# Retention scores of two heads as one 256-column product in high and low halves, with one transpose for both heads' keys

## The chip, the cores and the metric

The kernel runs on one core of a Trainium2 chip. A core has a matrix engine (TensorE, PE in the profile), a vector engine (VectorE, DVE), a scalar engine (ScalarE, ACT), GpSimd (POOL) and SyncE (SP), which here only issues DMAs. Each engine works through its own list in order and waits on semaphores. The metric is device microseconds of one execution; the median of three runs is compared.

## The reference

One encoder layer with 1,024 positions of width 1,024. After a modulated RMS norm one input projection feeds two groups of heads: eight retention heads and eight heads of latent attention. Both outputs go through one output projection and a gated residual. The change is in the retention. Its reference, cut to what matters:

```python
# q, k: (B,H,S,64) after rotary embedding, v: (B,H,S,128); chunks of 128 positions
scores = jnp.einsum('bhnik,bhnjk->bhnij', qc, kc) * decay_intra[None, :, None]
intra = jnp.einsum('bhnij,bhnjv->bhniv', scores, vc)
k_decay = jnp.exp(log_gamma[:, None] * (CHUNK - 1 - idx)[None])
kv_chunk = jnp.einsum('bhnjk,bhnjv->bhnkv', kc * k_decay[None, :, None, :, None], vc)
# states: scan over chunks; q_decay likewise
cross = jnp.einsum('bhnik,bhnkv->bhniv', qc * q_decay[None, :, None, :, None], states)
return (intra + cross).reshape(B, H, S, dv)
# run once forward (with the diagonal) and once on flipped sequences (without it), and added
```

## The kernel before

Data stay in fp32. Most products use a split: an operand is written as a high half (rounded to the matmul type fp32r) and a low half (the rest), and `mm3` (lines 64 to 67) adds three products, high by high, high by low and low by high. The small products of the retention were left as plain fp32 products, without a split.

The retention loop (lines 330 to 446) takes a pair of heads per pass `g`, four passes. A pass first makes eight tiles `t` of 128 positions. The projection of a tile is 24 products of 512 columns into a PSUM bank `acc` (line 343), giving q and k of both heads (4 x 64 columns) and v. VectorE and GpSimd apply the rotary embedding (lines 354 to 361) and write four blocks of 64 columns into every other row of `r_`, one of two buffers `rbuf` of eight rows: q of the two heads in rows 0 and 2, k in rows 4 and 6. The copy of line 362 doubles the q rows into rows 1 and 3; rows 5 and 7 stay zero.

Then per tile: `kd`, the keys scaled by the forward and the backward decay, in four instructions (line 366); four transposes of two rows each into one PSUM tile `tp` (line 370), giving q of each head twice on the 128 partitions, and k of each head over 64 zeros; a copy of all of it, `qkT` (line 372); `qdT`, q scaled by both decays (line 374); one plain fp32 score product per head (line 378), whose upper 64 partitions meet zeros of k; `sT`, scores times the mask (line 380); the state products of `kd` with v (line 385), added into the running states `ST` (lines 392 and 396). The PSUM tiles `tp`, `scp` and `kv` rotate over four banks (`sm`).

After the eight tiles the gate of the pair is projected (lines 404 to 414), and for each half of the sequence the outputs are made from `sT`, `qdT`, `ST` and v (lines 424 and 425), normalised (lines 430 to 438), transposed (line 442) and multiplied by the gate into `ro` (line 444), which SyncE stores.

`mla_gate` (lines 449 to 461) projects gates of the attention heads; its first two calls use the buffers of `qkT` for their results. The two calls follow the loop in the program, but are run beside its last pass.

The program order is not the order on the chip: when the program is built, a planner (`schedule_with_timeline_sim=True`) plays it through with its own estimate of each instruction's time and fixes every engine's list. So large products of the next tile or pair are listed between a tile's transposes and its scores. The order of the lists is fixed from then on, and an instruction at the head of a list that waits holds all behind it.

Of the kernel before, what the change touches and what calls it, by code (L numbers as in the profile page):

```python
# [18 lines left out]
P = 128  # L19
# [11 lines left out]
def body(tc, I, O):  # L31
# [291 lines left out]
    retD = dram.tile([H, P, S], F32, name="retD")  # L323
    mgD = dram.tile([H, P, S], F32, name="mgD")

    rbuf = [p_ret.tile([P, 8, 64], F32, name=f"rb{i}", tag=f"rb{i}") for i in range(2)]
    for b_ in rbuf:
        G.memset(b_, 0.0)

    for g in range(4):  # L330
        w = w0 if g == 0 else [wpage(I["w_ret"][g][j], 1024, 2) for j in range(4)]
        vv = []
        ST = p_ret.tile([P, NT, 2, P], F32, name="ST", tag="ST")
        sT = [None] * NT
        qdT = [None] * NT
        for t in range(NT):
            if g == 0 and t < NB0:
                ps = acc0[t]
            else:
                ps = acc()  # L340
                for k in range(KT):
                    wh, wl = w[k // 2]
                    mm3(ps, hh[k][:, ts_(t)], hl[k][:, ts_(t)], wh[:, k % 2], wl[:, k % 2], k == 0, k == KT - 1)
            v_ = p_ret.tile([P, 2, P], F32, name="v", tag="v", bufs=9)
            A.copy(out=v_.rearrange("p h d -> p (h d)"), in_=ps[:, 256:512])  # L345
            vv.append(v_)
            xq = ps[:, 0:256]
            if g == 0 and NACC <= t < NB0:
                xq = p_ret.tile([P, 256], F32, name="xq", tag="o", bufs=5)
                A.copy(out=xq, in_=ps[:, 0:256])  # L350
            xq = xq.rearrange("p (a d) -> p a d", d=32)
            t1 = p_ret.tile([P, 4, 2, 32], F32, name="t1", tag="t1", bufs=2)
            t2 = p_ret.tile([P, 4, 2, 32], F32, name="t2", tag="t2", bufs=2)
            V.tensor_tensor(out=t1.rearrange("p a b d -> p (a b) d"), in0=xq,
                            in1=Cr[:, t:t + 1].broadcast_to([P, 8, 32]), op=ALU.mult)
            V.tensor_tensor(out=t2.rearrange("p a b d -> p (a b) d"), in0=xq,
                            in1=Sr[:, t:t + 1].broadcast_to([P, 8, 32]), op=ALU.mult)
            r_ = rbuf[t % 2]
            rv = r_.rearrange("p (a z) d -> p a z d", z=2)[:, :, 0].rearrange("p a (b d) -> p a b d", b=2)
            G.tensor_tensor(out=rv[:, :, 0], in0=t1[:, :, 0], in1=t2[:, :, 1], op=ALU.subtract)  # L360
            G.tensor_tensor(out=rv[:, :, 1], in0=t1[:, :, 1], in1=t2[:, :, 0], op=ALU.add)
            V.tensor_copy(out=r_[:, 1:4:2], in_=r_[:, 0:4:2])
            kd = p_ret.tile([P, 2, 2, 64], F32, name="kd", tag="kd", bufs=2)
            for h in range(2):
                for d in range(2):
                    V.tensor_scalar(out=kd[:, h, d], in0=r_[:, 4 + 2 * h],
                                    scalar1=kfac[:, 2 * g + h, d:d + 1], scalar2=None, op0=ALU.mult)
            tp = sm(512)
            for a in range(4):
                T.transpose(tp[:, ts_(a)], r_[:, 2 * a:2 * a + 2].rearrange("p a b -> p (a b)"), ident)  # L370
            qkT_ = p_ret.tile([P, 4, P], F32, name="qkT", tag="qkT", bufs=2)
            A.copy(out=qkT_.rearrange("p a b -> p (a b)"), in_=tp)
            qdT_ = p_ret.tile([P, 2, P], F32, name="qdT", tag="qdT", bufs=8)
            V.tensor_tensor(out=qdT_, in0=tp[:, 0:256].rearrange("p (a b) -> p a b", a=2),
                            in1=qfac[:, 2 * g:2 * g + 2], op=ALU.mult)
            scp = sm(256)
            for h in range(2):
                T.matmul(scp[:, ts_(h)], qkT_[:, 2 + h], qkT_[:, h], start=True, stop=True)
            sT_ = p_ret.tile([P, 2, P], F32, name="sT", tag="sT", bufs=8)
            V.tensor_tensor(out=sT_, in0=scp.rearrange("p (h d) -> p h d", h=2), in1=mask[:, 2 * g:2 * g + 2],  # L380
                            op=ALU.mult)
            sT[t], qdT[t] = sT_, qdT_
            kv = sm(256)
            for h in range(2):
                T.matmul(kv[:, ts_(h)], kd[:, h].rearrange("p a b -> p (a b)"), v_[:, h], start=True, stop=True)
            kvv = kv.rearrange("p (h d) -> p h d", h=2)
            if t < NT - 1:
                if t == 0:
                    V.tensor_copy(out=ST[0:64, 1], in_=kvv[0:64])
                else:  # L390
                    for h in range(2):
                        V.scalar_tensor_tensor(out=ST[0:64, t + 1, h], in0=ST[0:64, t, h],
                                               scalar=gch[0:64, 2 * g + h:2 * g + h + 1], in1=kvv[0:64, h],
                                               op0=ALU.mult, op1=ALU.add)
            if t > 0:
                A.copy(out=ST[64:128, t - 1], in_=kvv[64:128])
        for t in range(NT - 2, 0, -1):
            for h in range(2):
                V.scalar_tensor_tensor(out=ST[64:128, t - 1, h], in0=ST[64:128, t, h],
                                       scalar=gch[64:128, 2 * g + h:2 * g + h + 1], in1=ST[64:128, t - 1, h],  # L400
                                       op0=ALU.mult, op1=ALU.add)


        wg = [wpage(I["w_rg"][g][j], 1024, 4) for j in range(2)]
        sg = p_ret.tile([P, 2, S], F32, name="sg", tag="sg")
        for h in range(2):
            for half in range(2):
                ps = acc()
                for k in range(KT):
                    wh, wl = wg[k // 4]  # L410
                    rh = hh[k][:, half * 512:half * 512 + 512]
                    rl = hl[k][:, half * 512:half * 512 + 512]
                    mm3(ps, wh[:, k % 4, ts_(h)], wl[:, k % 4, ts_(h)], rh, rl, k == 0, k == KT - 1)
                A.activation(sg[:, h, half * 512:half * 512 + 512], ps, AF.Silu)

        for half in range(2):
            mv = p_ret.tile([P, 4, 2, 2], F32, name="mv", tag="mv", bufs=2)
            ob = []
            for q in range(4):
                t = half * 4 + q  # L420
                op = sm(256)
                lo, hi = (64, 128) if t == 0 else (0, 64) if t == NT - 1 else (0, 128)
                for h in range(2):
                    T.matmul(op[:, ts_(h)], sT[t][:, h], vv[t][:, h], start=True, stop=False)  # L424
                    T.matmul(op[:, ts_(h)], qdT[t][lo:hi, h], ST[lo:hi, t, h], start=False, stop=True)  # L425
                o_ = p_ret.tile([P, 2, P], F32, name="o", tag="o", bufs=5)
                A.copy(out=o_.rearrange("p h d -> p (h d)"), in_=op)
                for h in range(2):
                    bs = p_ret.tile([P, 6], F32, name="bs", tag="bs", bufs=4)
                    V.bn_stats(out=bs, in_=o_[:, h])  # L430
                    V.bn_aggr(out=mv[:, q, h], in_=bs)
                ob.append(o_)
            rst = p_ret.tile([P, 4, 2], F32, name="rst", tag="rst", bufs=2)
            rstd(rst.rearrange("p a b -> p (a b)"), mv[:, :, :, 1].rearrange("p a b -> p (a b)"), 8)
            for q in range(4):
                for h in range(2):
                    V.tensor_scalar(out=ob[q][:, h], in0=ob[q][:, h], scalar1=mv[:, q, h, 0:1],
                                    scalar2=rst[:, q, h:h + 1], op0=ALU.subtract, op1=ALU.mult)
            for h in range(2):
                tp = sm()  # L440
                for q in range(4):
                    T.transpose(tp[:, ts_(q)], ob[q][:, h], ident)
                ro = p_ret.tile([P, 512], F32, name="ro", tag="ro", bufs=2)
                V.scalar_tensor_tensor(out=ro, in0=tp, scalar=gnw[:, 2 * g + h:2 * g + h + 1],
                                       in1=sg[:, h, half * 512:half * 512 + 512], op0=ALU.mult, op1=ALU.mult)
                SY.dma_start(out=retD[2 * g + h, :, half * 512:half * 512 + 512], in_=ro)
# [14 lines left out]
                A.dma_start(out=mgD[2 * n + h, :, sl], in_=mo)  # L461

    for n in range(MG0):
        mla_gate(n, p_ret, "qkT")
    rts.close()


# [498 lines left out]
```

## Time and profile before

| | |
|---|---|
| median of three runs | 1058.83 us (1058.5 to 1059.71) |
| the profiled execution | 1057.49 us, of which its span is 1055.3 us |
| mean granted TensorE clock | 0.988 of full speed |
| instructions | 15,223 |
| TensorE's busy time | 1018.1 us |
| retention loop | about 80 to 436 us of the span |

The span runs from the first to the last instruction that the profile shows. Times in rows are microseconds from the span's start. `PE` rows are matmuls, `PEld` rows their weight loads. A matmul's duration reaches into the next one's, so distances between starts tell what it holds the array for. A plain fp32 product is shown as two matmul instructions, a transpose and an fp32r product as one. In a group of instructions "x4" is their count, and in square brackets stands the idle time of the engine ahead of it and what ended it.

### The profile page before, as it was taken

The numbers are of one execution on the slowest core, as the hardware profiler recorded it, in microseconds if no ns is written. First come the engines' busy times: TensorE is split into PE (matmuls) and PEld (weight loads), VectorE is DVE, ScalarE is ACT, GpSimd is POOL, SyncE is SP. The second block draws the span as 40 slices with busy tenths as digits, with TensorE's granted clock in tenths as the row PEclk, the third lists the DMA queues.
The fourth block names the chain that finished last, engine by engine and source line by source line (L and its number), as shares of the span: only waits on it lengthen the run. The fifth ranks groups of instructions, "written<-read, shape, count | busy, mean of one in ns | idle before, by whom it ended". The sixth has DMA issues, their size and how long they took to land.

```text
span 1055.3 us, 15223 instructions
## 1 busy us (share of the span) xinstructions
PE 1018.1 (96%) x5736; PEld 888.3 (84%) x5736; DVE 581.4 (55%) x1390; ACT 426.0 (40%) x800; POOL 404.1 (38%) x311
## 2 busy tenths in 40 slices
PE   5899999999999999999999999989999999989998
PEld 4687887888888888998888889879889999878887
DVE  7996546444643534336302116777877777883342
ACT  6654213312321322124322006577767776772100
POOL 2233315213411411224633217943466555873210
PEclk8899999999999999999999999999999999998999
DMA  9721103101110212224654520100000000003522
GB/s 365 264 64 57 41 1 120 41 2 62 63 36 20 85 47 73 102 84 136 201 171 153 183 85 11 41 1 2 20 21 21 2 20 22 21 20 120 169 101 70
DMA packets 30744, 82.27 MB, mean 78 GB/s; under 512 B 3536, under 2 KB 4560, under 8 KB 30672
## 3 DMA queue, kind: packets, MB, share of 16 engines
q1 hardware_dynamic: 25920, 72.92, 20.4%
q10 hardware_dynamic: 4752, 8.39, 2.2%
q8 instruction: 45, 0.74, 0.3%
q14 instruction: 27, 0.22, 0.1%
HBM read 64.52 MB, written 16.78 MB: 77 GB/s over the span
## 4 chain that ended last, share of the span: by engine, by line
PE 82%; DVE 11%; DMA 2%; ACT 2%; issue 2%; POOL 2%; ACTq 0%; DVEq 0%; POOLq 0%
PE acc L65 13%; PE acc L66 13%; PE acc L67 13%; PE pt L739 4%; PE sp L65 4%; PE sp L66 4%; PE sp L67 4%; PE po L66 3%; PE po L67 3%; PE po L65 3%; DVE x L178 2%; DMA wa<-w_ada 2%; PE sm L425 2%; PE sm L424 1%; PE sm L65 1%
## 5 line engine op out<-in xcount | busy, mean ns | idle before, releaser
L81 POOL TENSOR_TENSOR wl<-wr,wh 128x1024 fp32r<-128x1024 f32 (+2 forms) x51 | 115.2, 2268 | 173.2 <-ACT wh L80 148.9
L65 PE MATMUL acc<-wh,hh 128*128 128x512 f32 (+2 forms) x352 | 130.8, 372 | 1.7 <-ACT hh L189 1.7
L66 PE MATMUL acc<-wl,hh 128*128 128x512 f32 (+2 forms) x352 | 130.3, 370 | 0.0
L67 PE MATMUL acc<-wh,hl 128*128 128x512 f32 (+2 forms) x352 | 126.4, 368 | 2.1 <-DVE hl L190 2.1
L725 POOL TENSOR_SCALAR pr<-pr,st 128x1024 f32<-128x1024 f32 x62 | 72.0, 1165 | 101.1 <-DVE st L724 75.5
L65 PE MATMUL acc<-hh,wh 128*128 128x512 f32 x256 | 101.0, 395 | 1.7 <-ACT v L345 1.7
L742 DVE TENSOR_TENSOR pl<-pt,ph 128x512 fp32r<-128x512 f32 x128 | 85.3, 683 | 31.2 <-ACT ph L741 31.1
L66 PE MATMUL acc<-hl,wh 128*128 128x512 f32 x256 | 100.9, 394 | 0.0
L67 PE MATMUL acc<-hh,wl 128*128 128x512 f32 x256 | 100.6, 393 | 0.0
L80 ACT CAST wh<-wr 128x1024 fp32r<-128x1024 f32 (+2 forms) x55 | 53.8, 982 | 104.1 <-PE sm L66 45.1
L741 ACT CAST ph<-pt 128x512 fp32r<-128x512 f32 x128 | 73.1, 591 | 26.6 <-PE pt L739 24.6
L720 DVE TENSOR_REDUCE st<-sp 128x1 f32<-128x1024 f32 x62 | 75.4, 1216 | 6.5 <-PE sp L67 6.4
L66 PE MATMUL po<-pl,vh 128*128 128x256 f32 x256 | 76.5, 299 | 2.1 <-DVE pl L742 2.0
L723 ACT ACTIVATE pr<-sp,st 128x1024 f32<-128x1024 f32 x62 | 69.5, 1121 | 20.8 <-DVE st L721 20.5
L65 PEld LDWEIGHTS acc<-wh,hh 128*128 128x128 f32 x352 | 67.2, 191 | 10.9 <-ACT hh L189 2.1
L67 PEld LDWEIGHTS acc<-wh,hl 128*128 128x128 f32 x352 | 66.0, 188 | 11.1 <-DVE hl L190 3.0
L66 PEld LDWEIGHTS acc<-wl,hh 128*128 128x128 f32 x352 | 67.3, 191 | 8.7
L739 PE MATMUL pt<-ident,pr 128*128 128x128 f32 x496 | 70.2, 274 | 4.0 <-DVE st L724 2.7
L65 PE MATMUL po<-ph,vh 128*128 128x256 f32 x256 | 73.3, 286 | 0.0
L67 PE MATMUL po<-ph,vl 128*128 128x256 f32 x256 | 72.8, 284 | 0.0
L360 POOL TENSOR_TENSOR rb<-t,t 128x128 f32<-128x128 f32 x32 | 14.8, 464 | 135.0 <-PE sm L370 73.4
L739 PEld LDWEIGHTS pt<-ident,pr 128*128 128x128 f32 x496 | 57.9, 141 | 8.5 <-issue 2.9
(353 smaller groups left out, 2474.2 us busy)
## 6 DMA issues: line engine op xcount, KB each, us to landing
x<-w_ada SPq DMA_DIRECT2D x16, 512.0 KB, 7.1
wr<-w_ret SPq DMA_DIRECT2D x16, 512.0 KB, 3.5
wr<-w_rg SPq DMA_DIRECT2D x8, 512.0 KB, 3.5
retD<-ro SPq DMA_DIRECT2D x16, 256.0 KB, 2.1
wr<-w_mg SPq DMA_DIRECT2D x8, 512.0 KB, 3.5
wa<-w_ada SPq DMA_DIRECT2D x8, 512.0 KB, 3.5
wr<-w_out SPq DMA_DIRECT2D x8, 512.0 KB, 4.5
wro<-retD SPq DMA_DIRECT2D x8, 512.0 KB, 3.9
```

Of the source, the lines that this page charges most:

```text
L65: T.matmul(out, lh, rh, start=first, stop=False, **kw)
L66: T.matmul(out, lh, rl, start=False, stop=False, **kw)
L67: T.matmul(out, ll, rh, start=False, stop=last, **kw)
L80: A.copy(out=hi, in_=raw)
L81: eng.tensor_tensor(out=lo, in0=raw, in1=hi, op=ALU.subtract)
L178: V.scalar_tensor_tensor(out=wa, in0=wa, scalar=1.0, in1=sc, op0=ALU.mult, op1=ALU.mult, accum_out=mp[:, i:i + 1])
L720: V.tensor_reduce(out=st_[:, 0:1], in_=sp, op=ALU.max, axis=AX.X)
L723: A.activation(pr, sp, AF.Exp, bias=st_[:, 1:2], scale=sc_, accum_out=st_[:, 2:3])
L725: G.tensor_scalar(out=pr, in0=pr, scalar1=st_[:, 3:4], scalar2=0.0, op0=ALU.mult, op1=ALU.add)
L739: T.transpose(tp[:, ts_(q)], pr[:, ts_(half * 4 + q)], ident)
L741: A.copy(out=ph[half][:, :, c_], in_=tv)
L742: V.tensor_tensor(out=pl[half][:, :, c_], in0=tv, in1=ph[half][:, :, c_], op=ALU.subtract)
```

## The change

Row 5 of `r_` now also gets a copy (of row 4, the first head's k; the copy of line 362 covers three rows), and the third transpose takes rows 5 and 6, so that both heads' k lie on one set of 128 partitions, the first head on the lower 64 and the second on the upper 64. The fourth transpose is gone. k is split into `kTh` and `kTl`. q is split per head into tiles of 256 columns, `qh_` and `ql_`, kept zero outside two blocks: the first head's q on the lower 64 partitions of the first 128 columns, the second head's on the upper 64 of the last 128. One `mm3` of 256 columns then gives both heads' scores. The keys' decays are applied in one instruction with broadcast operands. `qkT` is gone, the cleared buffers are the q tiles instead of `rbuf`, and the two early calls of `mla_gate` use the buffers of `ro`.

```diff
     rbuf = [p_ret.tile([P, 8, 64], F32, name=f"rb{i}", tag=f"rb{i}") for i in range(2)]
-    for b_ in rbuf:
-        G.memset(b_, 0.0)
+    qz = [[p_ret.tile([P, 2, P], F32R, name=f"qz{n}{i}", tag=f"qz{n}{i}") for n in "hl"] for i in range(2)]
+    for z_ in qz:
+        for b_ in z_:
+            G.memset(b_.bitcast(F32), 0.0)
...
-            V.tensor_copy(out=r_[:, 1:4:2], in_=r_[:, 0:4:2])
+            V.tensor_copy(out=r_[:, 1:6:2], in_=r_[:, 0:5:2])
             kd = p_ret.tile([P, 2, 2, 64], F32, name="kd", tag="kd", bufs=2)
+            V.tensor_tensor(out=kd, in0=r_[:, 4:7:2].unsqueeze(2).broadcast_to([P, 2, 2, 64]),
+                            in1=kfac[:, 2 * g:2 * g + 2].unsqueeze(3).broadcast_to([P, 2, 2, 64]), op=ALU.mult)
+
+            tp = sm(384)
             for h in range(2):
-                for d in range(2):
-                    V.tensor_scalar(out=kd[:, h, d], in0=r_[:, 4 + 2 * h],
-                                    scalar1=kfac[:, 2 * g + h, d:d + 1], scalar2=None, op0=ALU.mult)
-            tp = sm(512)
-            for a in range(4):
-                T.transpose(tp[:, ts_(a)], r_[:, 2 * a:2 * a + 2].rearrange("p a b -> p (a b)"), ident)
-            qkT_ = p_ret.tile([P, 4, P], F32, name="qkT", tag="qkT", bufs=2)
-            A.copy(out=qkT_.rearrange("p a b -> p (a b)"), in_=tp)
+                T.transpose(tp[:, ts_(h)], r_[:, 2 * h:2 * h + 2].rearrange("p a b -> p (a b)"), ident)
+            T.transpose(tp[:, ts_(2)], r_[:, 5:7].rearrange("p a b -> p (a b)"), ident)
             qdT_ = p_ret.tile([P, 2, P], F32, name="qdT", tag="qdT", bufs=8)
             V.tensor_tensor(out=qdT_, in0=tp[:, 0:256].rearrange("p (a b) -> p a b", a=2),
                             in1=qfac[:, 2 * g:2 * g + 2], op=ALU.mult)
+
+            kTh, kTl = (p_ret.tile([P, P], F32R, name=f"kT{n}", tag=f"kT{n}", bufs=1) for n in "hl")
+            A.copy(out=kTh, in_=tp[:, 256:384])
+            V.tensor_tensor(out=kTl, in0=tp[:, 256:384], in1=kTh, op=ALU.subtract)
+            qh_, ql_ = qz[t % 2]
+            for h in range(2):
+                hs = slice(64 * h, 64 * h + 64)
+                A.copy(out=qh_[hs, h], in_=tp[hs, ts_(h)])
+                V.tensor_tensor(out=ql_[hs, h], in0=tp[hs, ts_(h)], in1=qh_[hs, h], op=ALU.subtract)
             scp = sm(256)
-            for h in range(2):
-                T.matmul(scp[:, ts_(h)], qkT_[:, 2 + h], qkT_[:, h], start=True, stop=True)
+            mm3(scp, kTh, kTl, qh_.rearrange("p a b -> p (a b)"), ql_.rearrange("p a b -> p (a b)"), True, True)
...
     for n in range(MG0):
-        mla_gate(n, p_ret, "qkT")
+        mla_gate(n, p_ret, "ro")
```

## Rows read from the trace of the kernel before

**Rows 1.** The page's engine table: busy us (share of the span) and instructions.

```profile
PE 1018.1 (96%) x5736; PEld 888.3 (84%) x5736; DVE 581.4 (55%) x1390; ACT 426.0 (40%) x800; POOL 404.1 (38%) x311
```

**Rows 2.** Windows, one a pass: length, busy PE, PEld, DVE, ACT, POOL; clock; DMA.

```profile
80.00:172.00 92.00, 88.63 (x471) 74.68 (x469) 49.11 (x165) 27.78 (x57) 27.68 (x32) 1.00 0.13 39
...
260.00:347.00 87.00, 87.00 (x466) 74.17 (x465) 44.72 (x149) 21.86 (x41) 25.14 (x27) 1.00 0.15 49
```

**Rows 3.** All of TensorE's waits, 75 to 400 us: total, times, longest.

```profile
PE acc L65 <- ACT v L345: 1.7, 1, 1.7
PE sm L442 <- DVE o L437: 1.7, 2, 1.4
PE sm L378 <- ACT qkT L372: 0.7, 1, 0.7
```

**Rows 4.** Timeline of TensorE, two regular tiles: start, duration, instruction.

```profile
123.71 0.60 PE L370 MATMUL sm<-ident,rb 128*128 128x128 f32 x4
...
129.18 0.60 PE L378 MATMUL sm<-qkT 128*128 128x128 f32 x4
...
130.07 0.60 PE L370 MATMUL sm<-ident,rb 128*128 128x128 f32 x4
130.42 0.48 PE L67 MATMUL acc<-wh,hl 128*128 128x512 f32 x1
130.74 0.40 PE L65 MATMUL acc<-wh,hh 128*128 128x512 f32 x1
130.97 0.40 PE L66 MATMUL acc<-wl,hh 128*128 128x512 f32 x1
```

**Rows 5.** Timeline of TensorE, attention stage, fp32r products of 256 columns.

```profile
831.03 0.28 PE L65 MATMUL po<-ph,vh 128*128 128x256 f32 x1
...
831.74 0.28 PE L65 MATMUL po<-ph,vh 128*128 128x256 f32 x1
831.86 0.60 PE L739 MATMUL pt<-ident,pr 128*128 128x128 f32 x4
832.22 0.37 PE L66 MATMUL po<-pl,vh 128*128 128x256 f32 x1
832.42 0.29 PE L67 MATMUL po<-ph,vl 128*128 128x256 f32 x1
```

**Rows 6.** Timeline of TensorE, first two tiles of the second pair.

```profile
170.57 0.62 PE L370 MATMUL sm<-ident,rb 128*128 128x128 f32 x4
...
172.53 0.61 PE L378 MATMUL sm<-qkT 128*128 128x128 f32 x4
...
173.69 0.60 PE L370 MATMUL sm<-ident,rb 128*128 128x128 f32 x4
174.96 0.71 PE L378 MATMUL sm<-qkT 128*128 128x128 f32 x4 [0.68 <-ACT qkT L372]
```

**Rows 7.** Groups by line and shape, ScalarE and VectorE: busy us, mean ns.

```profile
L742 DVE TENSOR_TENSOR pl<-pt,ph 128x512 fp32r<-128x512 f32 x128 | 85.3, 683 | 31.2 <-ACT ph L741 31.1
...
L366 DVE TENSOR_SCALAR kd<-rb,kfac 128x64 f32<-128x64 f32 x128 | 45.1, 406 | 0.0
...
L372 ACT COPY qkT<-sm 128x512 f32<-128x512 f32 x32 | 18.8, 587 | 87.3 <-PE sm L370 87.3
...
L374 DVE TENSOR_TENSOR qdT<-sm,qfac 128x256 f32<-128x256 f32 x32 | 13.1, 408 | 0.5 <-ACT qkT L372 0.5
...
L427 ACT COPY o<-sm 128x256 f32<-128x256 f32 x32 | 11.5, 374 | 31.7 <-PE sm L425 28.8 <-DVE bs L430 1.1 <-issue 1.0
```

**Rows 8.** Timeline of VectorE: four slow scalings and what follows them.

```profile
267.64 3.22 DVE L366 TENSOR_SCALAR kd<-rb,kfac 128x64 f32<-128x64 f32 x4
270.79 0.41 DVE L374 TENSOR_TENSOR qdT<-sm,qfac 128x256 f32<-128x256 f32 x1
```

**Rows 9.** Timeline of TensorE in the same tile as those scalings.

```profile
266.92 0.60 PE L370 MATMUL sm<-ident,rb 128*128 128x128 f32 x4
...
272.39 0.60 PE L378 MATMUL sm<-qkT 128*128 128x128 f32 x4
```

## The prediction, made before any run of the changed kernel

> **What bounds the kernel now.** The first view to read is the engine table: TensorE is busy for 96% of the span, the next engine, VectorE, for 55% [rows 1]. An average can hide a stage with another limit, so the second view is the windows over the four passes of the retention loop, one pass a pair of heads. From the second pair on TensorE has no idle time at all, VectorE stands at about half and ScalarE at a quarter; the first window, 92.00 us with 88.63 busy, has some [rows 2]. The third view, who TensorE waited for between 75 and 400 us, says how much: 1.7, 1.7 and 0.7 us, 4.1 in all, and each of these waits lies at the start of the loop or at the change from the first pair to the second [rows 3]. So in this stage an instruction taken from TensorE's list shortens the kernel by the time it held the array, and an instruction on another engine costs nothing as long as its result is there before TensorE's list reaches the reader. Both halves of that sentence have to be priced.
>
> **The array time of the removed and added products.** A busy time can't be used here: matmuls overlap, and the durations of 0.60 for four are longer than their spacing. What counts is the distance between starts. In a regular tile the group scores, state products, transposes starts at 129.18 and the large products go on at 130.42, the second of them 0.32 us later instead of the usual 0.23 [rows 4]. From 129.18 to 130.74, less one large product (0.23), is 1.33 us for 12 instructions, 0.111 each; the starts inside the group say the same (129.18 and 130.07: 0.89 for eight). A plain fp32 score product stands as two instructions in the trace, so the two score products are four, 0.445 us, and one transpose is 0.111.
>
> The new score product is three fp32r products of 256 columns. The kernel has such ones in the attention stage: from 831.03 to 831.74 there are six steps, 0.118 each [rows 5]; three are 0.355 us. Mixing the two kinds has no price of its own beyond the late second start counted above: four transposes between 256-column products take from 831.86 to 832.42 less one step of 0.118, 0.44 us, again 0.111 each [rows 5]. A lower bound for a step is half of a 512-column step, 0.113, so 0.340 for three; an upper one is the single step of 0.20 behind transposes [rows 5], which would make 0.355 + 0.08. I take 0.355, the steady row with the same tile shape.
>
> So per tile the scores give 0.445 - 0.355 = 0.09 and the missing transpose 0.11, together 0.20 us. There are 4 x 8 = 32 tiles: **6.4 us** off TensorE's list, with 3.8 (the dear step) and 6.9 (the cheap step) as bounds.
>
> **The other engines' work.** ScalarE's one copy of 128x512 was 0.587 us; a copy of 128x256 is 0.374 [rows 7]. The difference, 0.213 per 256 columns, puts one of 128 columns at 0.267; three of them are 0.80 of busy time, +0.2 us a tile. On VectorE the same step from 0.408 (256 columns out of PSUM) to 0.683 (512) gives 0.27 for a 128-column subtraction; three are 0.81. The four scalings of the decayed keys cost 4 x 0.406 = 1.62 us a tile [rows 7]; the one broadcast product of 256 columns should be near the 0.408 row. The copy that doubles rows has 192 columns instead of 128, under 0.1 more. VectorE so changes by 0.41 + 0.81 + 0.1 - 1.62, about -0.3 us a tile. Neither engine comes near TensorE's 96%, so all this is costed at nothing in itself; TensorE's own products cover it, and without that cover it would be the chain below that counts. Four cleared tiles of 256 columns instead of two of 512 are the same number of columns on GpSimd, which is busy for 38% [rows 1]: nothing. The gate tiles that now share the buffers of the normalised outputs could make ScalarE wait for an output DMA, 2 to 3 us once; four accumulator banks cover that: nothing.
>
> **The added wait, and who stands behind it.** Before, the scores waited for one ScalarE copy. Now the first of the three products waits for both heads' high half, the second for the last subtraction, and the third for the low half of k. On VectorE these stand behind the decayed-query product: 0.41 + 3 x 0.27 = 1.22 us if nothing overlaps, against 0.59 for the copy: the chain from transposes to scores grows by **0.64 us**, and by nothing if the starts overlap well enough. Behind the waiting score product in TensorE's list stand the state products, the next tile's transposes (whose PSUM buffers follow), and then all large products.
>
> Is there room? In 30 of the 32 tiles the scores start 5.47 us after their transposes (123.71 and 129.18 in [rows 4]), the transposes take 0.45, so 5.0 us are left for a chain of about 1.3. The worst case seen is a tile in which the four scalings stood in front on VectorE and took 3.22 us, twice their mean of 1.62: the transposes start at 266.92, the decayed-query product at 270.79, and the scores at 272.39 [rows 8, 9]. With three subtractions, 0.81, behind 271.2, the new chain ends at 272.0, 0.4 us before it is needed. So in the regular pattern the wait stays hidden, though in such tiles only just.
>
> At the start of the second pair the room is gone. The scores follow 1.96 us behind the transposes in the first tile and 1.27 in the second, and there TensorE already waits 0.68 us for the copy [rows 6]. These two tiles I charge with the longer chain: 2 x 0.64 = **1.3 us** lost (bounds: nothing, and 2 x 1.3 if the scaling stands in front too).
>
> A rule bears on the hope that VectorE also gets rid of its slow tiles. Scalings of one size and form have a mean of 0.406 us, but took 3.22 for four in the tile above [rows 7, 8], so part of that time is a wait inside the instruction. The Trainium skill (GPSIMD Engine Reference, Key points) says that GpSimd shares its SBUF interfaces with VectorE and that instructions in a two-port mode, or with two SBUF inputs, contend. By that rule the new scaling, which reads keys and factors both from SBUF, can still be held once a tile, and the 4.1 us of waits would not go away; without it one might count them as an extra gain. I count none of them in the sum.
>
> **Sum.** -6.4 + 1.3 = -5.1 us. The profiled execution took 1057.49 us, 2.2 of them outside its span of 1055.3, and becomes 1052.4. The median of the three runs is 1058.83, 1.34 above that execution, and so the forecast for the median is **1053.7 us**, 0.5% faster. What a measurement here can tell from no change is about 0.2%, 2.1 us.
>
> **The rivals.**
>
> *Everything is got and the old waits go too.* Fewer VectorE instructions at the start of the second pair would remove the waits of 1.7 and 0.7 us for normalised outputs and the copy: -6.4 - 2.4 = -8.8, 1050.0 us. For it speaks the lighter VectorE, against it the rule above and the longer chain at just that place. Chance 0.13.
>
> *No change.* The order of each engine's list is made anew by the planner from its own idea of the times, and the chain from transposes to scores sets how soon the next tile's transposes can be listed. If it lets the scores follow their transposes as closely as in the second pair's first tiles in some ten tiles, ten times 0.64 gives back the 6.4 us; the same happens if the freed array time turns into waits for weights at the pair changes. Time 1056.7 to 1060.9. For it: TensorE did run dry at one pair change, and a loop whose tiles come later leaves less other work beside the outputs. Against it: at the other two pair changes no wait at all is seen [rows 3]. Chance 0.17.
>
> *Slower.* The same mechanism in every tile: scores right behind the transposes in all 32, each waiting 0.64 us longer: 20.5 - 6.4 = +14.1, 1072.9 us. It decides from 13 exposed tiles on (13 x 0.64 = 8.3, less 6.4, is +2). For it: small instructions on two engines that hand over to each other five times, where one copy stood. Against it: the distance of 5.47 us, the same in 30 tiles, leaves 3.7 to spare. Chance 0.10.
>
> *The change doesn't shorten the list*, because a step of 256 columns is dearer between plain fp32 products: the bound of 3.8 us, less 1.3, 1056.3. This lies at the edge of the forecast's own range and is counted in it.
>
> **How the numbers follow.** The forecast has 0.60; its own range is 1051 to 1056.5, from the bounds of the array time (3.8 to 6.9) and of the exposed tiles (0 to 2.6). With the first rival faster has 0.73, the same 0.17, slower 0.10. To leave out no more than 2 in 10 the range goes from 1050.2, where most of the first rival is outside, to 1058.9, past half of the no-change case.
>
> **What would show it.** In the changed kernel's profile: three transposes a tile (96 in all) and 96 score products of 256 columns, with 0.118 us between starts, the whole small group of a tile about 1.13 us instead of 1.33. The distance from transposes to scores should stay above 5 us in most tiles, and TensorE's waits for a subtraction or a small copy should sum to under 3 us. The windows of the later pairs should show TensorE as busy as before and be about 1.6 us shorter each. VectorE's busy time should fall by about 10 us, and ScalarE's rise by about 7. The prediction is wrong if score products show waits in many tiles, if the step is near 0.2, or if new idle time appears at the changes of pairs or in the latent projections after the loop.

## The result, and the profile after

The changed kernel took **1119.99 us** (median of 4 runs, 1119.24 to 1122.44) against 1059.27 for the kernel before on the same chip: a ratio of 1.0575 [1.0553, 1.0596], 5.8% slower where 0.5% faster was forecast. Its profiled execution spans 1120.5 us, 65.2 more than before.

The page's engine table of the changed kernel, to be held against [rows 1]:

```profile
PE 1037.8 (93%) x5672; PEld 899.8 (80%) x5672; DVE 586.6 (52%) x1390; ACT 430.2 (38%) x864; POOL 408.5 (36%) x313
```

TensorE has 64 instructions fewer and yet is busy 19.7 us longer, and its idle time, span less busy, rose from 37.2 to 82.7 us. The two together, 45.5 + 19.7, are the 65.2 us. Where they lie is in the windows over the retention stage of the changed kernel, cut as [rows 2]:

```profile
80.00:172.00 92.00, 85.70 (x424) 72.20 (x423) 43.96 (x143) 25.89 (x68) 22.20 (x27) 0.94 0.09 32
172.00:260.00 88.00, 79.38 (x378) 65.43 (x378) 39.71 (x117) 19.44 (x51) 23.21 (x24) 0.92 0.13 43
260.00:347.00 87.00, 77.39 (x378) 64.74 (x378) 34.61 (x120) 18.76 (x47) 25.10 (x24) 0.92 0.16 49
347.00:440.00 93.00, 83.85 (x425) 69.55 (x424) 44.09 (x143) 21.75 (x54) 25.05 (x25) 0.96 0.12 38
440.00:520.00 80.00, 63.94 (x322) 56.40 (x321) 23.34 (x88) 14.52 (x36) 10.15 (x11) 0.87 0.18 64
```

Every window has 6 to 16 us of idle, and the granted clock, 1.00 in the windows of [rows 2], is 0.87 to 0.96. No other engine has become the bound: VectorE stays under half of each window, ScalarE under 30%. So TensorE waits for something late, and the view of its waits, 75 to 520 us, says for what ([rows 3] had 4.1 us in all up to 400; up to 520 the kernel before has 5.9, the changed one 49.4):

```profile
PE sm L451 <- DVE o L446: 20.4, 6, 7.3
PE sm L65 <- ACT qzh L384: 12.9, 6, 2.7
PE acc L65 <- DVE t L359: 6.9, 3, 2.7
PE acc L65 <- ACT ro L469: 3.6, 1, 3.6
PE acc L65 <- ACT v L348: 2.1, 1, 2.1
PE acc L65 <- ACT sg L423: 2.1, 3, 0.7
PE sm L434 <- DVE ST L408: 0.8, 2, 0.4
PE sm L433 <- DVE sT L389: 0.6, 1, 0.6
```

The largest sum is not at the changed lines. It is the transposes of the normalised outputs, L451, in the output stage behind each pair's loop; the score products' own 12.9 us are six waits in the last tiles of the loops, as at 247.66 (2.70 us). In a regular tile nothing waits. This is one, from the timeline of the changed kernel, all engines, large products and weight loads left out:

```profile
121.01 0.28 PE L65 MATMUL sm<-qzh,kTh 128*128 128x256 f32 x1
...
121.78 0.42 DVE L389 TENSOR_TENSOR sT<-sm,mask 128x256 f32<-128x256 f32 x1 [4.71 <-PE sm L67]
121.80 0.38 PE L372 MATMUL sm<-ident,rb 128*128 128x128 f32 x2
...
122.02 0.27 PE L373 MATMUL sm<-ident,rb 128*128 128x128 f32 x1
...
122.64 0.53 DVE L367 TENSOR_TENSOR kd<-rb,kfac 128x256 f32<-128x256 f32 x1
...
123.09 0.41 DVE L375 TENSOR_TENSOR qdT<-sm,qfac 128x256 f32<-128x256 f32 x1
...
123.59 0.27 ACT L379 CAST kTh<-sm 128x128 fp32r<-128x128 f32 x1 [0.42 <-DVE qdT L375]
...
124.39 0.28 DVE L380 TENSOR_TENSOR kTl<-sm,kTh 128x128 fp32r<-128x128 f32 x1
...
124.70 0.26 ACT L384 CAST qzh<-sm 64x128 fp32r<-64x128 f32 x1 [0.85 <-DVE kTl L380]
...
125.00 0.28 DVE L385 TENSOR_TENSOR qzl<-sm,qzh 64x128 fp32r<-64x128 f32 x1 [0.33 <-ACT qzh L384]
...
125.31 0.26 ACT L384 CAST qzh<-sm 64x128 fp32r<-64x128 f32 x1 [0.35 <-DVE qzl L385]
...
125.61 0.29 DVE L385 TENSOR_TENSOR qzl<-sm,qzh 64x128 fp32r<-64x128 f32 x1 [0.33 <-ACT qzh L384]
...
129.85 0.28 PE L65 MATMUL sm<-qzh,kTh 128*128 128x256 f32 x1
```

Read it from the brackets. The copy of the keys' high half waits for the decayed queries (qdT), and the second copy of the queries' high half for the first head's low half: no data passes between them. What they have in common is that they read the same PSUM tile, `sm` from L372 and L373. (The two query copies also write one SBUF tile, `qzh`, which the subtraction between them reads; the run with the queries in SBUF, below, settles which of the two it is.) So seven readers stand in one row, ending at 125.90, 3.6 us behind the last transpose. The score products are listed another 3.95 us later, 8.05 us behind their transposes (5.47 in [rows 4]), and the next transposes only behind those. TensorE does not wait for the row here: on the chip the row is done 3.95 us before its reader starts, and it is the planner's list that puts the scores so far back. The distance between the score products of two tiles is thereby 8.84 us, where [rows 4] is part of a loop with 6.36. The tile's small group, on the other hand, did become shorter: from its start at 121.01 to the second large product behind it, at 122.36, less one large product, it takes 1.12 us, against 1.33 in [rows 4].

The Trainium skill (PSUM — Partial Sum Buffer, PSUM bank collisions raise a hardware error) says that two engines must not access one bank and 32-partition quadrant at the same time, two reads included, and that software has to keep them apart. By that rule the trace agrees for the keys' copy behind the decayed queries; the two heads' halves lie on different partitions, 0 to 63 and 64 to 127, so that wait goes further than the rule asks, and no run here lets the two engines read different partitions of one PSUM tile side by side.

**The theory** that I tested: in this loop a tile's row of readers is no slack but the period, since the transposes of the next tile are listed behind the scores of this one. Eight longer periods take the large products that stood beside the output stage, which is a chain of its own. **Rivals**: the mixed products cost more on the array; the one-instruction decayed keys and GpSimd hold each other up; the shared buffers of the gate's outputs (`ro`).

The order of TensorE's instructions in the program shows the mechanism without a time. This is the number of 512-column products from one tile's first transposes to the next tile's, in the second pair, and last from its eighth tile to the third pair's first (the kernels are those of the experiments below):

```
before                       0  16  22  22  22  22  22   136
changed                     22  30  34  36  34  32  28    72
before, row of seven        20  27  33  32  34  31  31    80
changed, qdT last            0  40  31  31  28  29  28   101
changed, q from SBUF         0  21  25  25  27  25  25   140
changed, grouped             0  22  22  22  22  22  22   136
```

A pair brings 288 such products (192 for the next pair's tiles, 96 for its gate), and the changed kernel's row adds up to just that (the rows of the kernel before and of the grouped one add up to 262 and 268: there some of the pair's products stand ahead of its first tile). What the loop takes, the output stage lacks: 136 become 72.

### The profile page after: what moved, and what is told of

It reads as the page before. It is cut to its first block, busy times and chain, and to the rows that moved or that the text cites. A ratio compares the mean times of both kernels' runs of the same rounds, so it can differ in the third digit from the quotient of the medians.

```text
span 1120.5 us, 15200 instructions
## 1 busy us (share of the span) xinstructions
PE 1037.8 (93%) x5672; PEld 899.8 (80%) x5672; DVE 586.6 (52%) x1390; ACT 430.2 (38%) x864; POOL 408.5 (36%) x313
## 4 chain that ended last, share of the span: by engine, by line
PE 49%; DVE 4%; DMA 2%; ACT 1%; POOL 1%; issue 1%; ACTq 0%; DVEq 0%; POOLq 0%
PE acc L65 5%; PE acc L66 5%; PE acc L67 5%; PE pt L748 4%; PE sp L65 4%; PE sp L66 4%; PE sp L67 4%; PE po L66 3%; PE po L67 3%; PE po L65 3%; DMA wa<-w_ada 2%; PE sm L67 1%; PE sm L66 1%; PE sm L65 1%; PE pt L661 1%
## 5 line engine op out<-in xcount | busy, mean ns | idle before, releaser
L81 POOL TENSOR_TENSOR wl<-wr,wh 128x1024 fp32r<-128x1024 f32 (+2 forms) x51 | 114.7, 2256 | 204.1 <-ACT wh L80 188.3
L65 PE MATMUL acc<-hh,wh 128*128 128x512 f32 x256 | 106.1, 415 | 14.6 <-DVE t L359 6.9
L66 PE MATMUL acc<-hl,wh 128*128 128x512 f32 x256 | 104.5, 408 | 0.0
L67 PE MATMUL acc<-hh,wl 128*128 128x512 f32 x256 | 103.7, 405 | 0.0
L65 PEld LDWEIGHTS acc<-hh,wh 128*128 128x128 f32 x256 | 50.7, 198 | 27.9 <-DVE t L359 7.8
```

The lines of the kernel that those rows point to most:

```text
L65: T.matmul(out, lh, rh, start=first, stop=False, **kw)
L66: T.matmul(out, lh, rl, start=False, stop=False, **kw)
L67: T.matmul(out, ll, rh, start=False, stop=last, **kw)
L81: eng.tensor_tensor(out=lo, in0=raw, in1=hi, op=ALU.subtract)
```

## The experiments

**The decayed keys alone, on the kernel before.**

```
-            for h in range(2):
-                for d in range(2):
-                    V.tensor_scalar(out=kd[:, h, d], ...)
+            V.tensor_tensor(out=kd, in0=r_[:, 4:7:2]..., in1=kfac[:, 2 * g:2 * g + 2]..., op=ALU.mult)
```

> The kernel before with one edit alone: the decayed keys in one VectorE instruction. Theory (the lost time comes from the longer row of readers of the transposes' PSUM tile, which this kernel does not have): the tile period of the loop stays at 6.36 us, the time is within 0.3% of before, 1056 to 1062 us, and VectorE's busy time falls by about 20 us. Rival (the one instruction, which reads two SBUF operands and took 632 ns on average in the changed kernel, holds VectorE and GpSimd up): 1075 us or more.

Measured: 1059.43 us, ratio 1.0005 [0.9997, 1.0014]: the same. The group of that line in this kernel:

```profile
L364 DVE TENSOR_TENSOR kd<-rb,kfac 128x256 f32<-128x256 f32 x32 | 19.5, 609 | 0.0
```

It is dearer than the 0.408 us predicted, but the four old ones kept VectorE busy for 1.41 us a tile (45.1 us for 32 tiles in [rows 7]), and VectorE's busy time fell from 581.4 to 563.2. The rival is out: this edit does not change the time.

**The row of readers alone, on the kernel before.** The same copies in total, cut into six that take turns; array work, products and buffers as before.

```
-            A.copy(out=qkT_..., in_=tp)
             V.tensor_tensor(out=qdT_, in0=tp[:, 0:256]..., ...)
+            for i, (c0, c1) in enumerate(((256, 384), (384, 512), (0, 64), (64, 128), (128, 192), (192, 256))):
+                (V.tensor_copy if i % 2 else A.copy)(out=qkf[:, c0:c1], in_=tp[:, c0:c1])
```

> The kernel before with its array work, its buffers and its plain fp32 score products untouched; only the copy of the transposes out of PSUM is cut into six pieces that ScalarE and VectorE make in turn, behind the decayed queries, so that seven readers of one PSUM tile stand in a row as in the changed kernel. Theory (that row sets the distance from a tile's transposes to its score products, and eight of them set the length of a pair of heads): the period of a tile rises from 6.36 us to 8 to 9 us, new idle stretches behind the output stage, 1100 to 1130 us. Rivals (the price of the mixed products on the array, the shared buffer of the gate's outputs, the one-instruction decayed keys): this kernel has none of them, so 1056 to 1064 us.

Measured: 1108.14 us, ratio 1.0463 [1.0446, 1.0480], +49.6 us. TensorE's waits in this kernel, 75 to 520 us, are headed by the same two readers as in the changed one (normalised outputs, and the last piece of the row):

```profile
PE sm L444 <- DVE o L439: 21.7, 3, 7.7
PE sm L380 <- DVE qkT L377: 4.6, 3, 2.3
```

Regular tiles follow each other by 8.85 us (VectorE's mask products at 207.49 and 216.34). All pieces together copy the same 512 columns; only their row is longer. That alone makes four fifths of the loss.

**The same instructions, grouped.** In the changed kernel, ScalarE's three copies first, then VectorE's three subtractions, then the decayed queries.

```
-            V.tensor_tensor(out=qdT_, ...)
             A.copy(out=kTh, in_=tp[:, 256:384])
-            V.tensor_tensor(out=kTl, ...)
-            for h in range(2): A.copy(out=qh_[hs, h], ...); V.tensor_tensor(out=ql_[hs, h], ...)
+            for h in range(2): A.copy(out=qh_[hs[h], h], ...)
+            V.tensor_tensor(out=kTl, ...)
+            for h in range(2): V.tensor_tensor(out=ql_[hs[h], h], ...)
+            V.tensor_tensor(out=qdT_, ...)
```

> The changed kernel with the same instructions in another order: ScalarE makes its three high copies one after the other, then VectorE the three low halves, then the decayed queries, so that the PSUM tile changes hands once before the scores instead of six times. Theory: the period of a tile falls from 8.85 us to 6.1 us (22 large products between transposes and scores instead of 34), the idle behind the output stages goes, and what the prediction counted appears: 1048 to 1062 us. Rivals (the price of the mixed products, contention of VectorE and GpSimd, the shared buffer, one buffer for the keys' halves): none of them is touched, so 1110 us or more.

Measured: 1067.83 us, ratio 1.0082 [1.0068, 1.0095]. Order alone gives 52 of the 61 us back, with every product and every cast of the changed kernel still there. But it is 6 us above the range I gave. A tile in TensorE's timeline of this kernel:

```profile
117.59 0.38 PE L372 MATMUL sm<-ident,rb 128*128 128x128 f32 x2
117.81 0.27 PE L373 MATMUL sm<-ident,rb 128*128 128x128 f32 x1
122.94 0.28 PE L65 MATMUL sm<-qzh,kTh 128*128 128x256 f32 x1
```

5.35 us from transposes to scores, and 6.15 us from tile to tile (scores at 116.79 and 122.94): 0.21 less than before, just the array time of the prediction. So the remainder is elsewhere. The windows of the first three pairs are about as full as before (88.47, 86.69, 87.00 us busy); the last is not, and TensorE's waits inside it say why:

```profile
347.00:440.00 93.00, 81.91 (x414) 68.63 (x413) 38.25 (x132) 20.71 (x50) 19.46 (x20) 0.94 0.16 56
```

```profile
PE sm L451 <- DVE o L446: 7.1, 2, 3.8
PE acc L65 <- ACT ro L469: 4.0, 1, 4.0
```

In the kernel before the same window was full:

```profile
347.00:440.00 93.00, 93.00 (x499) 80.14 (x498) 39.41 (x133) 23.84 (x45) 24.83 (x25) 1.00 0.24 80
```

There the gate's tiles are written from 387.63 on, within the last loop; here the first `ro` of the gate is written at 419.45, behind the last pair's outputs, whose buffers it shares. ScalarE stood idle until the store of such an output had landed:

```profile
419.45 0.60 ACT L469 ACTIVATE ro<-acc 128x512 f32<-128x512 f32 x1 [8.82 <-DMA retD<-ro]
```

**Two tiles under way.** The changed kernel with the row as it is, but a tile's scores behind the next tile's transposes; two buffers for kT, room for them by 7 slots in `rb` and one small buffer fewer. The shared `ro` stays.

```
+            def back(t=t, v_=v_, kd=kd, qdT_=qdT_, kTh=kTh, kTl=kTl, qh_=qh_, ql_=ql_):
                 scp = sm(256)
                 mm3(scp, kTh, kTl, ...)
...
+            if pend: pend.pop()()
+            pend.append(back)
+        pend.pop()()
```

> The changed kernel with the row of seven readers as it is, but each tile's scores and key-value products are issued after the next tile's transposes, with two buffers for the keys' halves (room for them by 7 instead of 8 slots in the rotated tile). Theory (what is lost is that one tile's row must end before the next tile's begins): two rows are under way at once, the distance from transposes to scores stays near 8 us but the period of a tile is no longer tied to it and falls under 7 us, 1045 to 1065 us. Rival (the instructions themselves cost it): 1110 us or more.

Measured: 1064.05 us (median of ten runs, 1057.39 to 1065.96), ratio 1.0039 [1.0021, 1.0058], inside the theory's range. The row is as long as ever: transposes that start at 189.24 have their scores at 196.51, 7.27 us later, with another tile's scores (191.90) in between. The eight mask products of the second pair lie between 175.10 and 207.84, 4.68 us apart on average. The same long row no longer sets the period once the next one need not wait for it.

**The shared buffers**, three ways: undone in the grouped kernel, undone alone in the changed kernel, and done alone in the kernel before.

```
# undone, in the grouped and in the changed kernel
-                mo = pool.tile([P, 512], F32, name=tag, tag=tag, bufs=2)
+                tg = tag[half] if isinstance(tag, tuple) else tag
+                mo = pool.tile([P, 512], F32, name=tg, tag=tg, bufs=1 if isinstance(tag, tuple) else 2)
...
-        mla_gate(n, p_ret, "ro")
+        mla_gate(n, p_ret, ("rb0", "rb1"))
# done alone, in the kernel before
-        mla_gate(n, p_ret, "qkT")
+        mla_gate(n, p_ret, "ro")
```

> The changed kernel with the readers grouped as in the experiment before, and with the gate's outputs of the loop after the retention in the buffers of the rotated tile, which are free when the last pair's tiles are done, instead of the buffers of the retention's outputs. Theory (of what is left above the kernel before, 11.1 us is TensorE idle in the last pair alone, 3.36, 3.78 and 3.95 us, because the gate's tiles have to wait until the last pair's outputs are written): the gate's tiles fill the last pair's output stage again, and what remains is the array time that the change saves: 1051 to 1058 us. Rival (the shared buffer costs nothing, as the prediction had it; the remainder is the price of the mixed products): 1064 to 1070 us.

> The changed kernel with nothing but the gate's outputs moved to the buffers of the rotated tile. Theory: the row of readers stays, so the tile period stays near 8.85 us in all four pairs, but the last pair's output stage is filled: the waits there, 2.2, 5.2, 3.7 and 3.6 us, go, with some of the stretch at the lower clock behind them: 1098 to 1108 us. Rival (the shared buffer costs nothing): 1117 to 1123 us.

> The kernel before with one edit alone: the gate's outputs share the buffers of the retention's outputs, as in the changed kernel. Theory (the gate's tiles can no longer be written before the last pair's outputs): about 11 us of new idle in the last pair, 1066 to 1075 us. Rival (the prediction's own step, the shared buffer costs nothing): 1056 to 1062 us.

Measured: **1052.07** us (0.9941 [0.9929, 0.9954]), 1101.09 (1.0399 [1.0383, 1.0415]) and 1072.02 (1.0130 [1.0116, 1.0144]), all inside the theory's ranges. The edit that the prediction costed at nothing is worth 13.6 us on the kernel before, 15.8 on the grouped one and 18.9 on the changed one. The last pair's window, first with `ro` on the kernel before, then in the grouped kernel without it:

```profile
347.00:440.00 93.00, 82.16 (x420) 69.46 (x419) 37.43 (x131) 20.99 (x39) 21.39 (x22) 0.93 0.18 58
```

```profile
347.00:440.00 93.00, 93.00 (x491) 80.43 (x490) 41.56 (x136) 24.04 (x59) 24.23 (x25) 1.00 0.24 80
```

10.84 us of idle come and go with it, and the clock with them. The grouped kernel with its own buffers beats both kernels.

**Grouped, own buffers, and two tiles under way.**

> Readers grouped, the gate's outputs in the rotated tile's buffers, and each tile's scores behind the next tile's transposes (one buffer for the keys' halves). Theory: with the row short enough TensorE is the limit again, and a second tile under way brings nothing more: the same as the kernel grouped without it, within 5 us, 1049 to 1060 us. Rival (the row of a tile still sets the time in the grouped kernel): 1045 us or less.

Measured: 1056.21 us, ratio 0.9981 [0.9972, 0.9990], inside the theory's range and 4 us behind the kernel without the second tile. But it does not test the theory. With one buffer for the keys' halves, the first step of a tile's row has to wait for the scores of the tile before. ScalarE's waits between 75 and 440 us are headed by just that, in 22 of the 32 tiles:

```profile
ACT kTh L378 <- PE sm L66: 61.6, 22, 5.2
```

So two rows were not under way at once, and whether the grouped kernel would gain from that is open.

**The decayed queries behind the row**, which keeps its turns.

```
-            V.tensor_tensor(out=qdT_, ...)
             A.copy(out=kTh, in_=tp[:, 256:384])
...
+            V.tensor_tensor(out=qdT_, ...)
             scp = sm(256)
```

> The changed kernel with one step of the row moved: the decayed queries are made behind the six copies and subtractions instead of ahead of them; these still take turns. Theory (the length of the row up to the scores sets the loss): the order of TensorE's instructions then has 28 to 31 large products between transposes and scores, against 34 in the changed kernel and 22 in the grouped one, so about half of what the grouping gave: 1088 to 1106 us. Rival (it is the turns of the engines that cost, each hand-over for itself, and the decayed queries are in none of the six): 1112 to 1122 us.

Measured: 1110.95 us, ratio 1.0490 [1.0472, 1.0509]: 9 us back instead of 14 to 32, a miss for the theory's size and outside the rival's range as well. The lengths of the second pair, from VectorE's mask products (first to eighth tile, and from there to the third pair's first), show why:

```
                        loop    output stage   pair
before                  43.6    42.8            86.3
changed                 57.4    45.8           103.2
changed, qdT last       53.3    45.9            99.2
before, row of seven    56.9    46.1           103.0
changed, grouped        42.2    43.5            85.7
```

The output stage of this pair takes 43 to 46 us whether it has 136 large products beside it or 72. So in the kernels without a second tile under way it acts as a chain, and a pair's time is the sum of two chains. The loop became 4.1 us shorter, not half of the 15: the products between transposes went from 34 only to 28 to 31, and a period from 8.2 to 7.6 us. In the third pair there was no gain (98.9 and 99.3 us). I had read the time off the number of products as if the first tiles and the change of pair did not count.

**The queries from an SBUF copy**, with room for it by 7 slots in `rb` and one small buffer fewer.

```
+            A.copy(out=qc, in_=tp[:, 0:256])
-            V.tensor_tensor(out=qdT_, in0=tp[:, 0:256]..., ...)
+            V.tensor_tensor(out=qdT_, in0=qc..., ...)
-                A.copy(out=qh_[hs, h], in_=tp[hs, ts_(h)])
+                A.copy(out=qh_[hs, h], in_=qc[hs, ts_(h)])
-                V.tensor_tensor(out=ql_[hs, h], in0=tp[hs, ts_(h)], in1=qh_[hs, h], op=ALU.subtract)
+                V.tensor_tensor(out=ql_[hs, h], in0=qc[hs, ts_(h)], in1=qh_[hs, h], op=ALU.subtract)
```

> The changed kernel with one instruction more: ScalarE copies the queries' half of the transposes' PSUM tile to SBUF once, and the decayed queries and the queries' high and low halves read that copy, in the old order and still taking turns in the program; only the copy and the keys' two steps read the PSUM tile. Theory (the engines take turns only because they read one PSUM tile; where the source is in SBUF a step waits for its own data alone): the row becomes shorter although it has more work, 24 to 25 large products between transposes and scores instead of 34, 1066 to 1090 us. Rival (what counts is the work of ScalarE and VectorE ahead of the scores): a little more than the changed kernel, 1118 us or more.

Measured: 1087.35 us, ratio 1.0281 [1.0247, 1.0316]: one copy more, and 33 us faster than the changed kernel (31 by the ratios, each to the kernel before on its own chip). ScalarE's timeline of this kernel, one regular tile:

```profile
194.29 0.37 ACT L376 COPY qc<-sm 128x256 f32<-128x256 f32 x1 [4.75 <-PE sm L374]
194.56 0.27 ACT L382 CAST kTh<-sm 128x128 fp32r<-128x128 f32 x1
194.85 0.37 ACT L408 COPY ST<-sm 64x256 f32<-64x256 f32 x1
195.25 0.62 ACT L387 CAST qzh<-qc 64x128 fp32r<-64x128 f32 x2
```

Both heads' high copies now follow each other without a wait for VectorE, in the same order of the program. They still write the one tile `qzh` that the subtractions read, so that was not the reason: it is the common PSUM tile that made the engines take turns.

**The kernel before with two tiles under way.** The edit of the fourth experiment on the kernel before.

> The kernel before with each tile's scores and key-value products issued behind the next tile's transposes, all else as it was. Theory (TensorE is the limit of the kernel before, its row of readers is just short enough to be covered): no gain, 1054 to 1064 us, with 12 to 24 products between transposes and scores instead of 22. Rival (the row sets the time of the kernel before as well, so that untying it gives time back): 1048 us or less.

Measured: 1053.92 us, ratio 0.9957 [0.9941, 0.9974]: between the two ranges. TensorE's waits for normalised outputs and the score copy (1.7 and 0.7 us in [rows 3]) are gone from its trace, and the windows of the second to fourth pair are full. So the row cost the kernel before at most a little, about 5 us; the rest of it was covered. Even these 5 us are not all shown to be the row's: in the profiled execution TensorE's idle time is only 1.2 us less than before (36.0 against 37.2), and its busy time 3.3 us less (1014.8 against 1018.1), for which no cause is shown.

## Why the prediction was wrong

**The step that failed is "Is there room?"** It took the 5.47 us from transposes to scores (5.47 in 28 tiles, 6.02 in two) for slack, of which 0.64 more could be used. But the distance is itself the period: the next tile's transposes are listed behind these scores, so 5.47 and the small group make up nearly all of the 6.36. The list is made anew for the changed kernel, and the prediction's sum kept the old one. When the row grew, the distance in the list grew to 8.05, with 34 large products in it instead of 22, and nothing in the regular tile waited. On the chip there was indeed room, 4.2 us before and 3.95 after, but an engine that follows a fixed list can't use it. "The distance should stay above 5 us" was the wrong sign to look for; it came true, and it was the loss. The last sign that it named, new idle time at the changes of pairs, was the right one. A row alone (+49.6 us on the kernel before), its regrouping (-52) and its untying (-56) show that.

**The row's length** was mis-sized as well. It was put at 1.22 us if nothing overlaps, 0.64 more than one copy. It counted VectorE's steps and left out ScalarE's in between, as well as VectorE's other work that slips into the gaps (L357, L359, L365); 3.6 us were measured, and 2.58 us between transposes and scores in the list.

**The rivals.** "Slower" and "no change" named the planner, and that "a loop whose tiles come later leaves less other work beside the outputs". That is what happened, but they were priced at 0.64 us a tile and at waits behind the transposes, 1072.9 at most.

**"Gate tiles that now share the buffers: nothing"** failed too. It looked for a wait of ScalarE on an output DMA, 2 to 3 us once, behind four accumulator banks. That wait came, and it was 8.6 us on the kernel before with this edit, 8.8 in the grouped one (419.45 above), because the store can only follow the last pair's outputs, which come at the end of the stage that the gate's products were to fill. The banks did not cover it: TensorE waited 3.7 us for it there, and 7.1 in the output stage without the filler; 13.6 us in all by the times.

**What was right** is the array time. Grouped, a tile is 0.21 us shorter (0.20 predicted), and with its own buffers the kernel takes 0.9941 of before, 6.2 us less, where -5.1 was forecast. That kernel is not the one forecast, and in its profiled execution TensorE's busy time is 3.8 us less and its idle time 1.5, so the 0.21 a tile is shown and the nearness of the two sums is in part luck. There are 96 transposes and 96 score products, and where three of them stand in a row they start 0.12 us apart (188.44, 188.56 and 188.68 in the kernel with two tiles under way). VectorE's busy time rose by 5.2 us instead of falling by 10, ScalarE's by 4.2 (7 predicted), neither of which mattered. Of the terms behind that, the four old scalings were 1.41 us of VectorE's time a tile and not 1.62 (4 x 0.406 counts their overlap twice; 45.1 us for 32 tiles stands in [rows 7]), the decayed keys took 0.632 instead of 0.408 us, the copy of rows 0.366 instead of 0.219 before; the small subtractions 0.287 and 0.288 (0.27 predicted).

**Where the 61 us are**, by the runs: about 50 for the row (+49.6 alone, 52 by regrouping), 14 to 19 for the shared buffers, less the 6 that the array saves. In the trace it is 45.5 us more of idle and 19.7 us more of busy TensorE, what the change saves on the array already taken off. That the slower products follow from the idle is read from the windows below, not tested by itself. **Open** is why the list keeps the scores about 4 us behind the end of the row (4.2 before, 3.95 changed, 3.3 grouped): no run changes the list and nothing else.

## What to carry to other kernels

Before reading a distance in a timeline as slack, ask what stands behind its far end: if the next tile's first step is listed behind this tile's last, the distance is the loop's period, and what lengthens it is paid in every tile, with no wait to be seen. Where a planner fixes the lists, count the instructions between the two in the new list before believing that the old distance stays. A stage without idle time may hold two chains of nearly the length of TensorE's work, and the place where the loss shows (here the output stage) is where the filler is missing, not where the edit was. When several engines read one PSUM tile, let each make all of its reads in one go, first those on the way to the next product; and give a tile that is to fill a gap buffers that are free before the gap.

## What the runs showed of the hardware

TensorE's granted clock fell where it had run dry. Three windows of the changed kernel in which it had waited: 7.28 us up to 283.88 in the first; 1.35, 2.10 and 5.18 up to 441.91, 445.40 and 457.80 in the second; 3.72 and 3.58 up to 469.21 and 474.99 in the third:

```profile
280.00:300.00 20.00, 13.78 (x55) 10.97 (x56) 8.65 (x27) 2.06 (x7) 5.51 (x6) 0.69 0.25 79
...
440.00:460.00 20.00, 11.24 (x62) 9.57 (x61) 11.21 (x48) 4.08 (x13) 3.26 (x3) 0.82 0.11 29
460.00:480.00 20.00, 12.70 (x51) 10.21 (x51) 9.03 (x32) 3.88 (x8) 1.84 (x2) 0.67 0.26 102
```

The large products behind the first of them start 0.42 us apart, against 0.23 in the regular tile, at a granted clock of 0.50 (290 to 292 us); that is the 1.2 GHz level:

```profile
288.25 0.79 PE L65 MATMUL acc<-hh,wh 128*128 128x512 f32 x1 [1.65 <-DVE t L359]
288.84 0.63 PE L66 MATMUL acc<-hl,wh 128*128 128x512 f32 x1
289.26 0.63 PE L67 MATMUL acc<-hh,wl 128*128 128x512 f32 x1
289.69 0.63 PE L65 MATMUL acc<-hh,wh 128*128 128x512 f32 x1
```

So idle time came with slower products behind it: 45.5 us more of idle with 19.7 us more of busy TensorE here. It is no fixed price: the row alone had 35.3 us of idle with 12.6, the shared buffers alone on the kernel before 7.8 with 6.4.

The one-instruction decayed keys took between 0.406 and 2.072 us for one shape, mean 0.632. The seven with no GpSimd instruction beside them took 0.41; the three longest (1.298, 1.847 and 2.072) all lay beside a GpSimd product of 1.8 to 2.4 us (L81, low halves of weights). The Trainium skill (GPSIMD Engine Reference, Key points), which has VectorE instructions with two SBUF inputs contend with GpSimd, fits that spread; by the run with this edit alone it changes nothing in the time.
